# One core, a gated hybrid layer: attention heads handled in pairs, the last projection in 256-column products

## The chip, the cores and the metric

The kernel runs on one core of one Trainium2 chip. Five engines work side by side, each through its own list of instructions in order: TensorE (PE in the profile) multiplies matrices into PSUM, VectorE (DVE), ScalarE (ACT) and GpSimd (POOL) do everything elementwise, and SyncE (SP) issues the transfers. They wait for one another through semaphores. The metric is the device time of one execution in microseconds (us).

## The reference

One layer on a sequence of 256 tokens with 1024 features. Cut to what the change touches: an attention of 8 heads with 128 features each (256 keys make one block, so every query sees its own block, causally), and the last projection.

```python
h = _rmsnorm(x, norm_w) * (1 + scale) + shift
(qa, ka, va, za, qm, km, vm, zm, om, ig, fg, ga, gm) = jnp.split(h @ w_in, SPLIT_IDX, axis=-1)
...
logit_own = jnp.einsum('bhqd,bhjd->bhqj', qc, k_own) * scale + bias_own
logit_own = jnp.where(dist_own >= 0, logit_own, NEG_INF)
p = jax.nn.softmax(...)
o = jnp.einsum('bhqj,bhjd->bhqd', p_own, v_own)
...
ya = (ya * jax.nn.silu(za)) @ w_att_proj
...
y = jax.nn.sigmoid(ga) * ya + jax.nn.sigmoid(gm) * ym
return x + gate * (y @ w_out)
```

The other branch, `ym`, is a chunked linear recurrence (mLSTM) with its own projection.

## The kernel before, in words

**The stream of products.** After a first phase that normalizes x and makes the columns of q and k (line 198), everything is one loop over 100 steps, `for g in range(NG)` at line 950. Four steps make one chunk of 344 or 512 output columns; step g multiplies two of the eight blocks of 128 input features. A weight w is split into a high and a low part in the format fp32r (`split`, line 441: ACT copies `wh`, DVE subtracts `wl`), and so is the activation, and each block takes three products: high by high, high by low, low by high. In "ws" chunks (lines 1001 to 1008) the weight is the stationary operand and 256 tokens are streamed, 24 products a step. In "tok" chunks (lines 994 to 999) the activation is stationary and 512 weight columns (344 for v) are streamed, 12 products a step. At the top of step g the parts of step g+4 are made; the ring of `wh` and `wl` has five buffers each.

**The attention in between.** It is put into the stream as calls hooked to steps. `between(g, ...)` runs a call inside `split` at step g, after the copy of `wh` and ahead of the subtraction of `wl`; `at(g, ...)` runs it after that. All their TensorE work stands ahead of the step's own products. For head h, with A0 = 10:

- `att_qk` (line 599), step 10+h: q times k in plain fp32 into an `aux` tile, then DVE adds the bias `Tb` and takes the row's extreme.
- `att_exp` (line 614), step 10+h: two exponentials on ACT.
- `att_norm` (line 620), step 11+h: DVE divides by the sums.
- `att_PT` (line 626), step 13+h: three 128x128 transposes on TensorE, and ACT copies them to `PT`.
- `att_av` (line 634), two heads a call, at steps 18, 20, 21 and 22: probabilities times v in fp32; then DVE multiplies by silu(za), and ACT and POOL split the result.

`aux` has four PSUM buffers, used in turn; a taker waits until the reader of the tile four takes earlier is done. `mm`, the products' own accumulators, has two. Each fp32 product with a 128-row operand shows as two MATMUL rows in the profile.

Steps 8 to 11 belong to the last v chunk, 12 to 19 to za, 20 to 43 to qm, km and the attention's projection; steps 44 to 67 are "tok" chunks of 512 columns. Other calls that sit in the stretch: transposes of q and k (`qk_T`) at steps 10 and 12, the mLSTM's gates at steps 10 to 21, of which `gates_T` (line 584) at step 18 transposes a tile of 36 rows.

**The last projection.** Chunk 23 (counted from 0), "out" (lines 985 to 992), multiplies y by the first 512 columns of w_out, 48 products of 512 columns over four steps. The last chunk (lines 1009 to 1018) is not in that loop: it goes by pieces, 512 columns for the first 128 tokens and two of 256 for the others, 24 products each, and each piece is evacuated (`ev_out`, line 855) and written out while the next is computed.

Of the kernel before, what the change touches and what calls it, by code (L numbers as in the profile page):

```python
# [17 lines left out]
KT = 8  # L18
AH, AD = 8, 128
# [47 lines left out]
def tile_hybrid(ctx: ExitStack, tc: tile.TileContext, x, c, params2, w_row, w_va, ada_mod, ada_gate,  # L67
                w_in, w_att_proj, w_ml_proj, w_out, out):
    nc = tc.nc
# [390 lines left out]
    def between(step, fn, *a):  # L460
        hooks_between.setdefault(step, []).append((fn, a))
# [421 lines left out]
    at(10, gates_2)  # L883
    at(12, qk_T, "k", 1)
    A0 = 10
    for h in range(AH):
        between(A0 + 1 + h, att_norm, h)
        between(A0 + h, att_qk, h)
        hooks_between.setdefault(A0 + 3 + h, []).insert(0, (att_PT, (h,)))
        at(A0 + h, att_exp, h)  # L890
    for step, fn in ((12, gates_3), (14, gates_copy), (15, gates_4), (17, gates_5), (18, gates_6), (18, gates_T),
                     (19, gates_7), (21, gates_D)):
        at(step, fn)
# [4 lines left out]
                at(s + q, lambda i, *a: conv(mmt[i], *a), C[nm, hf], hf, nm, q)  # L898
                at(s + q + 1, conv_silu, hf, nm, q)
    for q in range(2):  # L900
        at(done("za", 0) + 2 + 2 * q, att_av, 2 * q)
        at(done("za", 1) + 1 + q, att_av, 4 + 2 * q)
    s = 4 * C["zm", 0]
    for half in range(2):
        at(s + 5 * half, ml_split, half)
# [44 lines left out]
    for g in range(NG):  # L950
        ci, kp = divmod(g, 4)
        ch = chunks[ci]
        if g + A < NG:
            split(g + A, hooks_between.get(g, []))
            consumed.update(li for li in cons.get(g + A, []) if li not in gate_loads)
        if kp == 0:
            if ci > 0:
                pc = chunks[ci - 1]
                if pc["name"] in EV and ci - 1 != C["za", 0]:
                    EV[pc["name"]](mmt[ci - 1], pc["half"])  # L960
                elif pc["name"] == "out":
                    for t in range(2):
                        ev_out(mmt[ci - 1][:, t], pc["half"] * 512, 512, t)
            sh = [128, 2, 512] if ch["kind"] == "tok" else [128, 4, 256]
            if ci < NCH - 1:
                mmt[ci] = ps.tile(sh, F32, name="mm", bufs=2)
                if ch["kind"] == "tok":
                    mmt[ci] = mmt[ci][:, :, 0:ch["n"]]
        for fn, a in hooks.get(g, []):
            fn(*a)  # L970
        if g == A0 + AH - 1:
            ev_za(mmt[C["za", 0]], 0)
        if g in gate_left:
            consumed.add(gate_left[g])
        pump()
        if g == NG - 8:
            load_x()
        sh_, sl_ = (hTh, hTl) if ch["stat"] is None else (T[stat[ch["stat"]][0]], T[stat[ch["stat"]][1]])
        wh, wl = whl[g]
        if ci == NCH - 1:  # L980
            continue
        for kk in range(2):
            k = 2 * kp + kk
            first, last = k == 0, k == KT - 1
            if ch["name"] == "out":

                for i in (0, 1):
                    for t in range(2):
                        a = (sh_, sl_)[i][:, k, t * 128:(t + 1) * 128]
                        for w in (wh, wl)[:2 - i]:  # L990
                            nc.tensor.matmul(mmt[ci][:, t], a, w[:, kk], start=first and i == 0 and w is wh,  # L991
                                             stop=last and i == 1)
            elif ch["kind"] == "tok":
                for t in range(2):
                    a, b = sh_[:, k, t * 128:(t + 1) * 128], sl_[:, k, t * 128:(t + 1) * 128]
                    o = mmt[ci][:, t]
                    nc.tensor.matmul(o, a, wh[:, kk], start=first, stop=False)  # L997
                    nc.tensor.matmul(o, a, wl[:, kk], start=False, stop=False)  # L998
                    nc.tensor.matmul(o, b, wh[:, kk], start=False, stop=last)  # L999
            else:  # L1000
                for i in range(4):
                    cs = slice(i * 128, (i + 1) * 128)
                    o = mmt[ci][:, i]
                    nc.tensor.matmul(o, wh[:, kk, cs], sh_[:, k], start=first and i % 2 == 0, stop=False,  # L1004
                                     skip_group_check=True)
                    nc.tensor.matmul(o, wh[:, kk, cs], sl_[:, k], start=False, stop=False, skip_group_check=True)  # L1006
                    nc.tensor.matmul(o, wl[:, kk, cs], sh_[:, k], start=False, stop=last and i % 2 == 1,  # L1007
                                     skip_group_check=True)
    ci = NCH - 1
    for t, c0, n in ((0, 0, 512), (1, 0, 256), (1, 256, 256)):  # L1010
        pt = ps.tile([128, n], F32, name="mm", bufs=2)
        for k in range(KT):
            a, b = T["yh"][:, k, t * 128:(t + 1) * 128], T["yl"][:, k, t * 128:(t + 1) * 128]
            wh, wl = (w[:, k % 2, c0:c0 + n] for w in whl[4 * ci + k // 2])
            nc.tensor.matmul(pt, a, wh, start=k == 0, stop=False)  # L1015
            nc.tensor.matmul(pt, a, wl, start=False, stop=False)  # L1016
            nc.tensor.matmul(pt, b, wh, start=False, stop=k == KT - 1)  # L1017
        ev_out(pt, 512 + c0, n, t)


# [51 lines left out]
```

## Time and profile before

| | |
|---|---|
| three timed runs | 351.73, 352.65 and 352.78 us, median 352.65 |
| the profiled execution's own time | 351.62 us |
| its span, first to last instruction | 349.8 us |
| DVE, ACT, POOL busy | 246.5, 213.4, 91.6 us |
| from HBM | 76.14 MB, 221 GB/s over the span |

All times in the profile are counted from the span's start. The timeline lists start, duration, engine, line, operation, written and read tiles, and shape; rows of the same kind that follow one another are merged with their count (x2). A matmul's end is modelled, so durations of TensorE overlap: a 256-column product is shown with 0.28 us though the next one starts 0.11 us later. What a product costs is therefore read from the distance between starts, and this "pace" is used throughout.

### The profile page before, as it was taken

The numbers are of one execution on the slowest core, as the hardware profiler recorded it, in microseconds if no ns is written. First come the engines' busy times: TensorE is split into PE (matmuls) and PEld (weight loads), VectorE is DVE, ScalarE is ACT, GpSimd is POOL, SyncE is SP. The second block draws the span as 40 slices with busy tenths as digits, with TensorE's granted clock in tenths as the row PEclk, the third lists the DMA queues.
The fourth block names the chain that finished last, engine by engine and source line by source line (L and its number), as shares of the span: only waits on it lengthen the run. The fifth ranks groups of instructions, "written<-read, shape, count | busy, mean of one in ns | idle before, by whom it ended". The sixth has DMA issues, their size and how long they took to land.

```text
span 349.8 us, 6030 instructions
## 1 busy us (share of the span) xinstructions
PE 344.9 (99%) x2360; PEld 320.0 (91%) x2360; DVE 246.5 (70%) x369; ACT 213.4 (61%) x331; POOL 91.6 (26%) x81
## 2 busy tenths in 40 slices
PE   8999999999999999999999999999999999999996
PEld 7887889999999999999998888888899999999885
DVE  6999987976994436868866693864565875479951
ACT  4868789799777867676645654446556365534410
POOL 4800003941203362455004442000011320551000
PEclk9999999999999999999999999999999999999999
DMA  8999999990661544483975737559129129291011
GB/s 301 417 415 413 416 417 420 248 356 3 227 255 62 185 176 167 145 351 123 352 250 174 308 121 249 233 192 379 31 55 379 47 89 371 84 307 54 2 60 60
DMA packets 23515, 77.77 MB, mean 222 GB/s; under 512 B 3000, under 2 KB 4928, under 8 KB 22848
## 3 DMA queue, kind: packets, MB, share of 16 engines
q1 hardware_dynamic: 23336, 76.87, 59.5%
q10 hardware_dynamic: 152, 0.53, 0.5%
q8 instruction: 18, 0.29, 0.3%
q14 instruction: 9, 0.07, 0.1%
HBM read 76.14 MB, written 1.25 MB: 221 GB/s over the span
## 4 chain that ended last, share of the span: by engine, by line
PE 98%; ACT 1%; POOL 0%; DVE 0%; issue 0%; POOLq 0%
PE mm L1007 15%; PE mm L1006 15%; PE mm L1004 15%; PE pm L198 13%; PE mm L997 8%; PE mm L998 8%; PE mm L999 8%; PE mm L991 3%; PE xps L263 1%; PE mm L1017 1%; PE mm L1015 1%; PE aux L642 1%; PE mm L1016 1%; PE aux L492 1%; PE aux L604 1%; PE aux L762 1%
## 5 line engine op out<-in xcount | busy, mean ns | idle before, releaser
L452 DVE TENSOR_TENSOR wl<-raw,wh 128x1024 fp32r<-128x1024 f32 (+1 forms) x92 | 118.2, 1296 | 64.5 <-ACT wh L448 64.5
L448 ACT CAST wh<-raw 128x1024 fp32r<-128x1024 f32 (+1 forms) x100 | 100.5, 1014 | 54.8 <-PE mm L999 25.1
L1004 PE MATMUL mm<-hTh,wh 128*128 128x256 f32 x320 | 90.0, 281 | 0.0
L1006 PE MATMUL mm<-hTl,wh 128*128 128x256 f32 x320 | 88.7, 277 | 0.0
L1007 PE MATMUL mm<-hTh,wl 128*128 128x256 f32 x320 | 88.7, 277 | 0.0
L1004 PEld LDWEIGHTS mm<-hTh,wh 128*128 128x128 f32 x320 | 60.3, 188 | 0.0
L1006 PEld LDWEIGHTS mm<-hTl,wh 128*128 128x128 f32 x320 | 60.2, 188 | 0.0
L1007 PEld LDWEIGHTS mm<-hTh,wl 128*128 128x128 f32 x320 | 60.1, 188 | 0.0
L997 PE MATMUL mm<-wh,hTh 128*128 128x512 f32 (+1 forms) x144 | 53.0, 368 | 0.0
L998 PE MATMUL mm<-wl,hTh 128*128 128x512 f32 (+1 forms) x144 | 52.6, 365 | 0.0
L999 PE MATMUL mm<-wh,hTl 128*128 128x512 f32 (+1 forms) x144 | 52.6, 365 | 0.0
L999 PEld LDWEIGHTS mm<-wh,hTl 128*128 128x128 f32 x144 | 27.0, 188 | 3.8
L997 PEld LDWEIGHTS mm<-wh,hTh 128*128 128x128 f32 x144 | 27.1, 188 | 3.6
L998 PEld LDWEIGHTS mm<-wl,hTh 128*128 128x128 f32 x144 | 27.1, 188 | 3.5
L452 POOL TENSOR_TENSOR wl<-raw,wh 128x1024 fp32r<-128x1024 f32 x8 | 19.5, 2459 | 18.4 <-ACT wh L448 12.1
L183 ACT CAST wrh<-raw 128x512 fp32r<-128x512 f32 (+1 forms) x24 | 18.2, 761 | 7.4 <-DMA raw<-in_w_row_dram 7.4
L188 DVE TENSOR_TENSOR wrl<-raw,wrh 128x512 fp32r<-128x512 f32 (+1 forms) x26 | 20.5, 811 | 1.0 <-ACT wrh L183 1.0
L198 PE MATMUL pm<-wrh,hTh 128*128 128x512 f32 x64 | 19.9, 392 | 0.0
L198 PE MATMUL pm<-wrh,hTl 128*128 128x512 f32 x64 | 19.9, 392 | 0.0
L198 PE MATMUL pm<-wrl,hTh 128*128 128x512 f32 x64 | 18.9, 394 | 0.0
L1007 PE MATMUL mm<-yah,wl 128*128 128x256 f32 x64 | 17.7, 276 | 0.0
L1004 PE MATMUL mm<-yah,wh 128*128 128x256 f32 x64 | 17.7, 276 | 0.0
(218 smaller groups left out, 644.6 us busy)
## 6 DMA issues: line engine op xcount, KB each, us to landing
raw<-in_w_in_dram SPq DMA_DIRECT2D x32, 1024.0 KB, 5.2
adat<-in_ada_mod_dram SPq DMA_DIRECT2D x16, 512.0 KB, 8.8
raw<-in_w_va_dram SPq DMA_DIRECT2D x6, 688.0 KB, 9.2
raw<-in_ada_gate_dram SPq DMA_DIRECT2D x4, 1024.0 KB, 6.2
raw<-in_w_att_proj_dram SPq DMA_DIRECT2D x4, 1024.0 KB, 5.0
raw<-in_w_ml_proj_dram SPq DMA_DIRECT2D x4, 1024.0 KB, 5.4
raw<-in_w_out_dram SPq DMA_DIRECT2D x4, 1024.0 KB, 6.3
raw<-in_w_row_dram SPq DMA_DIRECT2D x15, 256.0 KB, 8.1
```

Of the source, the lines that this page charges most:

```text
L183: copy(wsp[k][0][:, c0:c1], wrow[k][:, c0:c1])
L188: e.tensor_tensor(l[:, cs], wrow[k][:, cs], h[:, cs].bitcast(F32), op=OP.subtract)
L198: nc.tensor.matmul(pm[ch][:, t], a[:, k, t * 128:(t + 1) * 128], b[:, cs], start=k == 0 and i == 0, stop=k == KT - 1 and i == 2)
L448: nc.scalar.copy(h, w)
L452: e.tensor_tensor(l, w, h.bitcast(F32), op=OP.subtract)
L991: nc.tensor.matmul(mmt[ci][:, t], a, w[:, kk], start=first and i == 0 and w is wh, stop=last and i == 1)
L997: nc.tensor.matmul(o, a, wh[:, kk], start=first, stop=False)
L998: nc.tensor.matmul(o, a, wl[:, kk], start=False, stop=False)
L999: nc.tensor.matmul(o, b, wh[:, kk], start=False, stop=last)
L1004: nc.tensor.matmul(o, wh[:, kk, cs], sh_[:, k], start=first and i % 2 == 0, stop=False, skip_group_check=True)
L1006: nc.tensor.matmul(o, wh[:, kk, cs], sl_[:, k], start=False, stop=False, skip_group_check=True)
L1007: nc.tensor.matmul(o, wl[:, kk, cs], sh_[:, k], start=False, stop=last and i % 2 == 1, skip_group_check=True)
```

## The change

Three edits.

1. The heads go in pairs. For h = 0, 2, 4, 6 both heads' `att_qk` and `att_exp` come at step 10+h, both `att_norm` at step 11+h, both `att_PT` at step 14+h; where transposes and new q-k products share a step, the transposes come first.
2. `att_av` is called for heads 0 to 3 at step 20 and for 4 to 7 at step 22 (before: 18, 20, 21, 22).
3. In the last projection, each product of 512 streamed columns becomes two of 256, into the two halves of the same bank.

```diff
     A0 = 10
-    for h in range(AH):
-        between(A0 + 1 + h, att_norm, h)
-        between(A0 + h, att_qk, h)
-        hooks_between.setdefault(A0 + 3 + h, []).insert(0, (att_PT, (h,)))
-        at(A0 + h, att_exp, h)
+    for h in range(0, AH, 2):
+        for fn, d in ((att_PT, 4), (att_qk, 0), (att_norm, 1)):
+            for hh in (h, h + 1):
+                between(A0 + h + d, fn, hh)
+        for hh in (h, h + 1):
+            at(A0 + h, att_exp, hh)
+    for i in range(A0 + 4, A0 + AH + 4, 2):
+        hooks_between[i].sort(key=lambda f: f[0] is not att_PT)
...
     for q in range(2):
-        at(done("za", 0) + 2 + 2 * q, att_av, 2 * q)
-        at(done("za", 1) + 1 + q, att_av, 4 + 2 * q)
+        at(done("za", 1), att_av, 2 * q)
+        at(done("za", 1) + 2, att_av, 4 + 2 * q)
...
                 for i in (0, 1):
-                    for t in range(2):
+                    for t, c0 in ((0, 0), (0, 256), (1, 0), (1, 256)):
                         a = (sh_, sl_)[i][:, k, t * 128:(t + 1) * 128]
+                        cs = slice(c0, c0 + 256)
                         for w in (wh, wl)[:2 - i]:
-                            nc.tensor.matmul(mmt[ci][:, t], a, w[:, kk], start=first and i == 0 and w is wh,
-                                             stop=last and i == 1)
+                            nc.tensor.matmul(mmt[ci][:, t, cs], a, w[:, kk, cs],
+                                             start=first and i == 0 and c0 == 0 and w is wh,
+                                             stop=last and i == 1 and c0 > 0, skip_group_check=True)
...
-            wh, wl = (w[:, k % 2, c0:c0 + n] for w in whl[4 * ci + k // 2])
-            nc.tensor.matmul(pt, a, wh, start=k == 0, stop=False)
...
+            for c1 in range(0, n, 256):
+                wh, wl = (w[:, k % 2, c0 + c1:c0 + c1 + 256] for w in whl[4 * ci + k // 2])
+                o = pt[:, c1:c1 + 256]
+                nc.tensor.matmul(o, a, wh, start=k == 0 and c1 == 0, stop=False, skip_group_check=True)
...
```

On TensorE, ahead of the products of step 13, one head's transposes and one head's q-k product stood in a row (three transposes of head 0 from its probabilities `P`, then the two products of head 3):

```order
L1007 MATMUL mm_952<-hTh_70,wl_818 128x256
L629 MATMUL aux_1000<-ident_65,P_877 128x128
L630 MATMUL aux_1000<-ident_65,P_877 128x128
L631 MATMUL aux_1000<-ident_65,P_877 128x128
L604 MATMUL aux_1008<-kT_629,qT_600 128x256
L605 MATMUL aux_1008<-kT_629,qT_600 128x128
L1004 MATMUL mm_952<-hTh_70,wh_854 128x256
```

Now step 13 has none of it, and ahead of the products of step 14 stand two heads of each (0 and 1, then 4 and 5), with four `aux` tiles taken in a row:

```order
L1012 MATMUL mm_959<-hTh_70,wl_855 128x256
L629 MATMUL aux_1045<-ident_65,P_877 128x128
L630 MATMUL aux_1045<-ident_65,P_877 128x128
L631 MATMUL aux_1045<-ident_65,P_877 128x128
L629 MATMUL aux_1050<-ident_65,P_884 128x128
L630 MATMUL aux_1050<-ident_65,P_884 128x128
L631 MATMUL aux_1050<-ident_65,P_884 128x128
L604 MATMUL aux_1055<-kT_629,qT_600 128x256
L605 MATMUL aux_1055<-kT_629,qT_600 128x128
L604 MATMUL aux_1062<-kT_629,qT_600 128x256
L605 MATMUL aux_1062<-kT_629,qT_600 128x128
L1009 MATMUL mm_959<-hTh_70,wh_870 128x256
```

At step 18 TensorE had one head's transposes, the gates' two transposes of 36 rows (L587), and the first two heads of probabilities times v:

```order
L631 MATMUL aux_1245<-ident_65,P_1106 128x128
L587 MATMUL aux_1256<-ident_65,GE_1114 128x36 x2
L642 MATMUL aux_1263<-PT_873,vat_729 128x256
L644 MATMUL aux_1263<-PT_873,vat_729 128x128
L642 MATMUL aux_1263<-PT_873,vat_729 128x256
L644 MATMUL aux_1263<-PT_873,vat_729 128x128
L1004 MATMUL mm_1163<-hTh_70,wh_1044 128x256
```

Now the step's own products follow the gates' transposes directly; the products with v have gone to step 20, behind the transposes of heads 6 and 7:

```order
L631 MATMUL aux_1248<-ident_65,P_1065 128x128
L587 MATMUL aux_1256<-ident_65,GE_1112 128x36 x2
L1009 MATMUL mm_1170<-hTh_70,wh_1042 128x256
```

In the out chunk, each stationary block of y (`yh`, `yl`) was followed by 512-column products; a block of input features took these rows on TensorE:

```order
L991 MATMUL mm_3544<-wh_3402,yh_3406 128x512
L991 MATMUL mm_3544<-wl_3403,yh_3406 128x512
L991 MATMUL mm_3544<-wh_3402,yh_3406 128x512
L991 MATMUL mm_3544<-wl_3403,yh_3406 128x512
L991 MATMUL mm_3544<-wh_3402,yl_3407 128x512 x2
```

Now it takes twice as many of half the width, the same stationary block loaded for each:

```order
L995 MATMUL mm_3544<-wh_3402,yh_3406 128x256
L995 MATMUL mm_3544<-wl_3403,yh_3406 128x256
L995 MATMUL mm_3544<-wh_3402,yh_3406 128x256
L995 MATMUL mm_3544<-wl_3403,yh_3406 128x256
...
L995 MATMUL mm_3544<-wh_3402,yl_3407 128x256 x4
```

More of the change, by code (lines that the diff above doesn't have):

```diff
@@ L1013, in tile_hybrid @@
             a, b = T["yh"][:, k, t * 128:(t + 1) * 128], T["yl"][:, k, t * 128:(t + 1) * 128]
-            wh, wl = (w[:, k % 2, c0:c0 + n] for w in whl[4 * ci + k // 2])
-            nc.tensor.matmul(pt, a, wh, start=k == 0, stop=False)
-            nc.tensor.matmul(pt, a, wl, start=False, stop=False)
-            nc.tensor.matmul(pt, b, wh, start=False, stop=k == KT - 1)
+            for c1 in range(0, n, 256):
+                wh, wl = (w[:, k % 2, c0 + c1:c0 + c1 + 256] for w in whl[4 * ci + k // 2])
+                o = pt[:, c1:c1 + 256]
+                nc.tensor.matmul(o, a, wh, start=k == 0 and c1 == 0, stop=False, skip_group_check=True)
+                nc.tensor.matmul(o, a, wl, start=False, stop=False, skip_group_check=True)
+                nc.tensor.matmul(o, b, wh, start=False, stop=k == KT - 1 and c1 + 256 == n, skip_group_check=True)
         ev_out(pt, 512 + c0, n, t)
```

## The prediction

> **What bounds the kernel now.** I read the page first, then TensorE's waits, then the timeline of TensorE row by row.
>
> ```profile
> span 349.8 us, 6030 instructions
> PE 344.9 (99%) x2360; PEld 320.0 (91%) x2360; DVE 246.5 (70%) x369; ACT 213.4 (61%) x331; POOL 91.6 (26%) x81
> PEclk9999999999999999999999999999999999999999
> PE 98%; ACT 1%; POOL 0%; DVE 0%; issue 0%; POOLq 0%
> PE warm L227 <- POOL ident masks.py:199: 1.4, 1, 1.4
> PE xps L263 <- ACT diag L246: 0.2, 1, 0.2
> ```
>
> The first four rows are the page's: TensorE is busy for 99% of the span, at 90% or more of its clock in every slice, and it holds 98% of the chain that ended last. The last two are the whole answer on TensorE's waits: 1.6 us, both in the first microseconds. So no attention call and no weight split is waited for longer than the view can show; the time is the sum of the distances between TensorE's starts. A change pays only if it shortens those, or costs if it makes TensorE wait. Busy time says nothing here, since modelled ends overlap; I use starts.
>
> **The last projection.** The rows are starts from the timeline, and groups with their counts.
>
> ```profile
> 324.12 0.39 PE L991 MATMUL mm<-wh,yh 128*128 128x512 f32 x1
> 340.88 0.28 PE L1015 MATMUL mm<-wh,yh 128*128 128x256 f32 x1
> 346.21 0.28 PE L1017 MATMUL mm<-wh,yl 128*128 128x256 f32 x1
> L991 PE MATMUL mm<-wh,yh 128*128 128x512 f32 x16 | 6.3, 394 | 0.0
> L1015 PE MATMUL mm<-wh,yh 128*128 128x512 f32 x8 | 3.1, 393 | 0.0
> L1015 PE MATMUL mm<-wh,yh 128*128 128x256 f32 x16 | 4.4, 276 | 0.0
> 211.34 0.40 PE L997 MATMUL mm<-wh,hTh 128*128 128x512 f32 x1
> 244.00 0.28 PE L779 MATMUL aux<-vaug,SD 128*128 128x258 f32 x1
> L997 PE MATMUL mm<-wh,hTh 128*128 128x512 f32 x48 | 18.7, 389 | 0.0
> ```
>
> Each group row is one of three alike (high by high, low, high), so between 324.12 and 340.88 lie 3 x 16 + 3 x 8 = 72 products of 512 columns: 16.76 / 72 = 0.2328 us each. From 340.88 to 346.21 the last two pieces start 3 x 16 = 48 products of 256 columns, 47 distances: 5.33 / 47 = 0.1134 us each. These take the same `wh`, `wl`, `yh` and `yl` tiles as the piece before, so the nearest row for the new form is in this very stage: two halves at 0.2268 against 0.2328. The last three rows say that 512 columns need not be slower: in the longest uninterrupted run of them, 3 x 48 = 144 products take 32.66 us, 0.2268 each, exactly two halves. The out stage is off that pace by 0.006, for a reason that the trace doesn't name. **Saving: 72 x 0.006 = 0.43 us**, all of it on the path, since nothing but TensorE holds the end there. Between ends: halves also run at a worse pace, 0.118 (shown below), which would give 0.236 a pair and 72 x 0.0032 = 0.23 us lost. I take the tail's row, the nearest.
>
> The Trainium skill, "TensorE: Matmul & The Clock Gate", Back-to-back issue gap, speaks against this edit: alone, a warm matmul's gap is N / 2.4 ns and about 2.5 ns more, whatever the width; so 72 more products would cost 72 x 2.5 ns = 0.18 us by it, an estimate. The rows above do not agree: 0.1134 is more than its 0.109, and twice it is no more than a whole. That rule's result is a rival below, priced from rows.
>
> **The attention's groups.** Thirteen steps, 10 to 22, have fp32 work ahead of their products; afterwards seven have (10, 12, 14, 16, 18, 20, 22). The number of products and transposes is the same, so only what each change of kind costs can go. Step 19 shows it alone, three transposes and 24 products:
>
> ```profile
> 109.36 0.27 PE L629 MATMUL aux<-ident,P 128*128 128x128 f32 x1
> 109.47 0.27 PE L630 MATMUL aux<-ident,P 128*128 128x128 f32 x1
> 109.58 0.27 PE L631 MATMUL aux<-ident,P 128*128 128x128 f32 x1
> 109.61 0.37 PE L1004 MATMUL mm<-hTh,wh 128*128 128x256 f32 x1
> 109.81 0.28 PE L1006 MATMUL mm<-hTl,wh 128*128 128x256 f32 x1
> 112.43 0.27 PE L629 MATMUL aux<-ident,P 128*128 128x128 f32 x1
> ```
>
> Transposes stand 0.11 apart. The last is followed after only 0.03, and the first product takes 0.20 in place of 0.1134: 0.08 early, 0.09 late. Read singly the 0.20 looks like a stop of 0.09 at each return to the stream, thirteen times; taken together it is mostly a matter of where the start is stamped. The whole step takes 112.43 - 109.36 = 3.07 us against 3 x 0.11 + 24 x 0.1134 = 3.05. **One group costs 0.02 us, six fewer save 0.12.** The ends: nothing, if the 0.02 is rounding, and 6 x 0.09 = 0.54, if the 0.20 is a stop after all.
>
> Step 18 is the one group with more:
>
> ```profile
> 104.76 0.27 PE L631 MATMUL aux<-ident,P 128*128 128x128 f32 x1
> 104.96 0.31 PE L587 MATMUL aux<-ident,GE 36*128 36x36 f32 x2
> 105.20 0.70 PE L642 MATMUL aux<-PT,vat 128*128 128x256 f32 x2
> 105.74 0.38 PE L644 MATMUL aux<-PT,vat 128*128 128x128 f32 x2
> 104.39 0.42 ACT L565 ACTIVATE GE<-G 4x256 f32<-4x256 f32 x1 [0.88 <-DVE st L622]
> 116.89 0.59 PE L642 MATMUL aux<-PT,vat 128*128 128x256 f32 x2
> 117.33 0.39 PE L644 MATMUL aux<-PT,vat 128*128 128x128 f32 x2
> ```
>
> The gates' transposes start 0.20 after L631 rather than 0.11, right after ACT ended L565 at 104.81: a wait of 0.09. They then hold 0.24, and the first pair of L642 takes 0.54, where in step 21 (116.89 to 117.33) it takes 0.44. The products with v leave this place, the gates' transposes stay. L565 hangs on DVE work of step 17, which now has no q-k product to wait for, but two heads to normalize; it comes as late relative to TensorE, I judge. So 0.09 of wait stays, and the 0.10 behind goes or moves to the step's own products. I count 0, with the ends 0.19 gained and 0.1 lost (the wait twice as long).
>
> On this the Trainium skill, "TensorEngine Tiling (Array Packing)", Key Properties, says that a change of tiling mode drains TensorE. Only L587 has 36 rows; by that rule the entry and the exit are paid before and after alike, which is the 0 that I count.
>
> **What the moves could make late.** No moved call issues a DMA. POOL gets the gates' copy and masks ahead of the first `yal`, which the projection at step 36 needs. What TensorE needs of the moved calls comes earlier: transposes of a pair follow its products by four steps, where each head had three.
>
> ```profile
> 84.93 0.28 DVE L624 TENSOR_SCALAR P<-P,st 128x128 f32<-128x128 f32 x1
> 89.62 0.27 PE L629 MATMUL aux<-ident,P 128*128 128x128 f32 x1
> 75.50:125.00 49.50, 49.50 (x397) 48.46 (x396) 33.95 (x80) 39.75 (x79) 14.69 (x14) 1.00 0.45 161
> ```
>
> Head 1 was normalized at 85.2 and transposed at 89.62, 4.4 us later, with three steps between; with four it has a step (2.8 us) more, less the other head's 0.8 on DVE and 0.9 on ACT. The four `aux` tiles of step 14 were last read two steps before. The last row (length; busy us of PE, its weight loads, DVE, ACT, POOL) has DVE busy for 34 and ACT for 40 of 49.5 us, so two heads at a time fit. **Cost: 0.** If that cover were gone, each microsecond of a late tile would stop all that is queued behind on TensorE, one for one.
>
> **The sum.** -0.43 - 0.12 = -0.55 us: 351.62 becomes 351.07 for the profiled execution (span 349.8 to about 349.25, with the same 1.82 around it). That execution is 1.03 below the median of the three runs; against 352.65 the forecast is **352.1 us**.
>
> **A term that can't be summed: the pace after a group.**
>
> ```profile
> 268.61 0.28 PE L1006 MATMUL mm<-hTl,wh 128*128 128x256 f32 x1
> 276.97 0.60 PE L816 MATMUL aux<-ident,omt 128*128 128x128 f32 x4
> 122.37 0.28 PE L1006 MATMUL mm<-hTl,wh 128*128 128x256 f32 x1
> 182.11 0.40 PE L997 MATMUL mm<-wh,hTh 128*128 128x512 f32 x1
> 86.91 0.28 PE L1006 MATMUL mm<-hTl,wh 128*128 128x256 f32 x1
> ```
>
> After the group that ends at 268.41, 71 products take 8.36 us, 0.1177 each, until the next group; after the one of step 22, 527 take 59.74, 0.1134. Same form, nothing waited for: the stream falls into one of two paces when it is re-entered, a close one and a wide one, and keeps it. Step 13 (86.91 to 89.62, 23 products) has the wide pace too, at 0.1178. Of the eleven 256-column steps 12 to 22, I read three as wide throughout (12, 13, 20). A wide step costs 24 x 0.0043 = 0.10 us. With new groups the draw is new: all three going close would gain 0.3 (and up to 0.1 more in the v chunk), three more wide steps lose as much. I count 0.
>
> **The rivals.**
> - *The wide pace catches the long run.* After step 22 there is no other group until step 47 and the width stays the same through 22 steps. If this entry falls on the wide side and stays there, 22 x 0.10 = 2.2 us are lost: 354.3. For it: about one entry in four is wide, and 72 products in a row never healed. Against it: this very entry was close, as were most with products with v before it. It decides from six wide steps (0.55 / 0.10), and ends clearly slower from sixteen. Chance 0.10.
> - *The halves run at the wide pace*: +0.23 for -0.43, so 352.65 + 0.23 - 0.12 = 352.8. For it: the 512-column products of this stage are off pace now. Against it: the tail's 47 distances, on the same tiles. 0.12.
> - *Each product has a price of its own*, the rule above. Rows bound it: a half at 0.1134 and a whole at 0.2268 leave 0.0001 at most, 72 x 0.0001 = 0.01 us; if the out stage's 0.006 is owed to something else and stays, the sum is +0.01 - 0.12: 352.5. 0.08.
> - *The groups cost nothing*, and pairing does not do what fewer groups suggest: only -0.43, 352.2. 0.15.
> - *The gain is larger*: a stop of 0.09 at each return (-0.54 in place of -0.12) or the wide steps gone (-0.4): 351.65. 0.13.
> - The forecast itself, 352.1: 0.42.
>
> **How the numbers follow.** A measurement of this kernel tells about 0.3%, 1.06 us, from no change. The forecast is half of that. The four executions shown, all of one kernel, lie in two pairs one microsecond apart (351.62 and 351.73, 352.65 and 352.78), so a median can fall on either, and that alone carries part of the forecast's chance to "faster": 0.12 of its 0.42 and the near rivals, and 0.08 of the larger gain, 0.20. Slower is the long run's 0.10 and 0.01 of the rest. The range goes from the larger gain on the lower of the pairs, 351.0, to the halves' rival on a high one, 353.2; the long run at the wide pace (0.10) and the far low end stay outside.
>
> **What would show each step.** In the new profile the first L995 to the last piece's first product should span 16.3 us, not 16.76, with pairs 0.227 apart; at 0.236 the second rival holds. From the first product of step 10's group to the end of step 22, 0.1 to 0.2 us should go, with steps 11, 13, 15, 17, 19 and 21 free of any 0.20. TensorE's waits should still list the first two rows alone; a third one, on ACT or DVE between 75 and 125 us, proves the cover wrong. And the distance from step 22's first product to the first 512-column product should be 59.9 us; 62 is the wide pace. The prediction is wrong if the time leaves the range, and wrong in its reasons if the out stage does not shorten.

## The result and the profile after

The changed kernel takes **355.09 us** (median of 22 runs, 352.77 to 358.0), the kernel before 351.88 beside it (22 runs, 351.3 to 353.14): ratio 1.0076, 95% interval 1.006 to 1.0092. It is slower by 0.8%, where 352.1 was forecast. The profiled execution took 355.62 us, 4.0 more than that of before.

These rows answer to the first ones shown of before: two of the page, then all that the view of TensorE's waits holds (microseconds in total, times, longest).

```profile
span 353.8 us, 6176 instructions
PE 347.2 (98%) x2432; PEld 325.2 (92%) x2432; DVE 246.5 (70%) x369; ACT 212.8 (60%) x331; POOL 90.0 (25%) x81
```

```profile
PE aux L587 <- ACT GE L565: 1.7, 1, 1.7
PE warm L227 <- POOL ident masks.py:199: 1.4, 1, 1.4
PE xps L263 <- ACT diag L246: 0.3, 1, 0.3
```

A third wait has come: TensorE stops for 1.7 us ahead of the gates' transposes of step 18. That is less than half of 4.0, so I cut the span at starts. First the row of before that the prediction did not show, then the timeline of TensorE after, with the start and the modelled length in front.

```profile
75.50 0.38 PE L604 MATMUL aux<-kT,qT 128*128 128x256 f32 x1
```

```profile
75.88 0.38 PE L604 MATMUL aux<-kT,qT 128*128 128x256 f32 x1
104.88 0.27 PE L631 MATMUL aux<-ident,P 128*128 128x128 f32 x1
106.83 0.31 PE L587 MATMUL aux<-ident,GE 36*128 36x36 f32 x2 [1.68 <-ACT GE L565]
107.07 0.39 PE L1009 MATMUL mm<-hTh,wh 128*128 128x256 f32 x1
124.32 0.36 PE L1009 MATMUL mm<-hTh,wh 128*128 128x256 f32 x1
186.59 0.39 PE L1002 MATMUL mm<-wh,hTh 128*128 128x512 f32 x1
328.60 0.28 PE L995 MATMUL mm<-wh,yh 128*128 128x256 f32 x1
350.25 0.28 PE L1024 MATMUL mm<-wh,yl 128*128 128x256 f32 x1
```

| stretch | before | after | difference |
|---|---|---|---|
| start to step 10's group | 75.50 | 75.88 | +0.38 |
| from there to the first product after step 22's group | 46.67 | 48.44 | +1.77 |
| the 528 products of steps 22 to 43 (the long run) | 59.94 | 62.27 | +2.33 |
| step 44 to the out stage | 142.01 | 142.01 | 0 |
| out stage, first to last product | 22.09 | 21.65 | -0.44 |
| behind the last product | 3.59 | 3.58 | -0.01 |

The first row is start-up, which lies between 75.40 and 76.19 us in the eighteen profiles, all of programs that are alike there. Two things cost: a stop, and a wider pace (62.27 / 528 = 0.118 us per product in place of 0.1135). The halves gained what was forecast.

**Why the stop.** L587 transposes `GE`, which ACT writes at L565. These are ACT's rows around it, then DVE's.

```profile
101.48 0.51 ACT L616 ACTIVATE P<-P,st 128x256 f32<-128x256 f32 x1 [1.80 <-DVE st L608]
102.87 0.39 ACT L617 ACTIVATE P<-P,st 128x128 f32<-128x128 f32 x1
103.26 1.03 ACT L448 CAST wh<-raw 128x1024 fp32r<-128x1024 f32 x1
106.36 0.41 ACT L565 ACTIVATE GE<-G 4x256 f32<-4x256 f32 x1 [2.07 <-DVE G L564]
```

```profile
100.39 0.68 DVE L559 TENSOR_TENSOR_SCAN G<-GE 4x256 f32<-4x256 f32 x1
100.99 0.39 DVE L608 CUSTOM_DVE_ANT_0 P<-aux,Tb 128x256 f32<-128x256 f32 x1
104.33 0.28 DVE L624 TENSOR_SCALAR P<-P,st 128x128 f32<-128x128 f32 x1
104.53 1.22 DVE L452 TENSOR_TENSOR wl<-raw,wh 128x1024 fp32r<-128x1024 f32 x1
105.66 0.27 DVE L563 TENSOR_SCALAR G<-G 4x256 f32<-4x256 f32 x1
105.86 0.41 DVE L564 TENSOR_TENSOR G<-G 4x256 f32<-4x256 f32 x1
```

Followed backwards: L565 waits 2.07 us for DVE's L564. That stands in DVE's order behind a weight split (L452, 1.22 us) and the norms of two heads (the last at 104.33). The split needs the cast that ACT starts at 103.26, behind the exponentials of two heads (from 101.48), and these need DVE's L608, issued behind a scan of the gates. The view by windows has the length, then busy time and count of PE, its weight loads, DVE, ACT and POOL, then the granted clock (and the DMA's share and rate):

```profile
95.30:105.90 10.60, 9.85 (x84) 9.51 (x82) 10.04 (x29) 7.15 (x20) 0.00 (x0) 1.00 0.78 296
```

DVE is busy for 10.04 of these 10.60 us, so what stands in front of L564 delays it in full, and two heads' work stands where one head's stood. L565 starts 1.97 us later than before (104.39), while TensorE comes only 0.12 later (104.88 against 104.76), after a start-up that was 0.38 later.

**Why the times spread.** Before spans 1.8 us, the changed kernel 5.2. Each execution comes with its mean granted clock, and times and clocks together make four groups:

| long run | mean clock 0.998 to 1.0 | mean clock 0.993 to 0.995 |
|---|---|---|
| close pace | 7 runs, 352.77 to 353.79 | 3 runs, 353.92 to 354.12 |
| wide pace | 8 runs, 355.04 to 356.19 | 4 runs, 356.87 to 358.0 |

Close and wide are told by time here; the two executions of this program with a profile (355.62 above, and 352.77 in an experiment below) bear it out. So 12 of 22 went at the wide pace, and 7 of 22 had a clock that was reduced for a while; the median is a wide run.

### The profile page after: what moved, and what is told of

Its sections match the earlier page's. It is cut to its first block, busy times and chain, and to the rows that moved or that the text cites. A ratio compares the mean times of both kernels' runs of the same rounds, so it can differ in the third digit from the quotient of the medians.

```text
span 353.8 us, 6176 instructions
## 1 busy us (share of the span) xinstructions
PE 347.2 (98%) x2432; PEld 325.2 (92%) x2432; DVE 246.5 (70%) x369; ACT 212.8 (60%) x331; POOL 90.0 (25%) x81
## 4 chain that ended last, share of the span: by engine, by line
PE 95%; DVE 2%; ACT 1%; issue 0%; POOL 0%; POOLq 0%; DVEq 0%; ACTq 0%
PE mm L1009 14%; PE mm L1011 14%; PE mm L1012 14%; PE pm L198 13%; PE mm L1002 8%; PE mm L1003 8%; PE mm L1004 8%; PE mm L995 3%; PE xps L263 1%; PE mm L1024 1%; PE mm L1023 1%; PE mm L1022 1%; DVE wl L452 1%; PE aux L492 1%; PE aux L642 1%; PE aux L762 1%
## 5 line engine op out<-in xcount | busy, mean ns | idle before, releaser
L452 DVE TENSOR_TENSOR wl<-raw,wh 128x1024 fp32r<-128x1024 f32 (+1 forms) x92 | 117.6, 1290 | 66.4 <-ACT wh L448 66.3
L452 POOL TENSOR_TENSOR wl<-raw,wh 128x1024 fp32r<-128x1024 f32 x8 | 19.5, 2457 | 19.0 <-ACT wh L448 19.0
```

The lines of the kernel that those rows point to most:

```text
L452: e.tensor_tensor(l, w, h.bitcast(F32), op=OP.subtract)
```

## The experiments

Steps are counted as in the prediction. All ratios are to the kernel before, run on the same chip beside it. "Close" and "wide" say how the long run was in the profile.

| kernel | median (range; runs) | ratio, interval | steps 10-22 | long run | out stage |
|---|---|---|---|---|---|
| halves alone (e1) | 351.88 (351.28-352.74; 11) | 0.9995, 0.9984-1.0007 | 46.68 | 59.95 | 21.65 |
| attention alone (e2) | 354.93 (353.99-357.3; 6) | 1.0092, 1.0066-1.0118 | 48.24 | 62.27 | 22.09 |
| gates' transposes at 20 (e3) | 354.46 (353.12-356.22; 6) | 1.008, 1.0056-1.0103 | 46.66 | 59.94 | 21.72 |
| pairs, v as before (e4) | 353.63 (352.57-355.16; 10) | 1.0037, 1.0014-1.0061 | 48.06 | 59.95 | 21.65 |
| the changed kernel again (g1) | 352.77 (1) | | 48.24 | 59.94 | 21.65 |
| before, gates at 17 (g2) | 356.3 (356.07-357.51; 4) | 1.0129, 1.0103-1.0154 | 52.52 | 59.94 | 22.09 |
| a group at step 24 (g3) | 353.45 (352.85-356.2; 10) | 1.0065, 1.004-1.009 | 48.22 | 60.28 | 21.65 |
| e4 with gates at 20 (g4) | 352.52 (352.38-352.75; 10) | 1.0016, 1.0007-1.0026 | 46.31 | 59.95 | 21.72 |
| gates_5 at 16 (h1) | 353.72 (353.4-354.58; 6) | 1.0051, 1.0033-1.0068 | 46.69 | 62.27 | 21.65 |
| e4 with gates_5 at 16 (h2) | 351.26 (350.67-352.54; 12) | 0.9989, 0.9975-1.0003 | 46.31 | 59.95 | 21.65 |
| e1 with gates at 20 (h3) | 350.99 (350.86-351.32; 10) | 0.9975, 0.9965-0.9984 | 46.68 | 59.95 | 21.65 |
| g4 with a group at 78 (h4) | 352.78 (352.61-353.73; 10) | 1.0029, 1.0017-1.0041 | 46.31 | 59.95 | 21.72 |
| single heads, v as changed (k1) | 353.86 (353.58-353.9; 5) | 1.0042, 1.0023-1.0062 | 46.96 | 62.27 | 21.65 |
| h1, last v call alone (k2) | 351.2 (351.06-352.14; 10) | 0.9979, 0.9969-0.999 | 46.60 | 59.95 | 21.65 |
| h1 again (k3) | 353.89 (1) | | 46.69 | 62.27 | 21.65 |
| e3 again (k4) | 355.75 (1) | | 46.85 | 62.27 | 21.72 |

### The halves alone (e1)

The attention lines are those of before; the last projection is the changed one.

```diff
-    for h in range(0, AH, 2):
...
+    for h in range(AH):
+        between(A0 + 1 + h, att_norm, h)
+        between(A0 + h, att_qk, h)
+        hooks_between.setdefault(A0 + 3 + h, []).insert(0, (att_PT, (h,)))
+        at(A0 + h, att_exp, h)
...
-        at(done("za", 1), att_av, 2 * q)
-        at(done("za", 1) + 2, att_av, 4 + 2 * q)
+        at(done("za", 0) + 2 + 2 * q, att_av, 2 * q)
+        at(done("za", 1) + 1 + q, att_av, 4 + 2 * q)
```

> The attention of before, only the last projection in halves. Theory A (the loss sits in the attention's stretch alone; the halves run at the close pace): the out stage spans 16.3 us instead of 16.76, TensorE's waits list the first two rows alone, the time is 0.44 us below before, 351.4. Rival B (more, smaller products cost time somewhere, for instance by the pace they are left in): same as before or up to 0.2 us more.

The timeline of TensorE has the first and the last product of the out stage:

```profile
324.83 0.28 PE L992 MATMUL mm<-wh,yh 128*128 128x256 f32 x1
346.48 0.28 PE L1021 MATMUL mm<-wh,yl 128*128 128x256 f32 x1
```

The stage takes 21.65 against 22.09: -0.44, shown on the path. The median moved by 0.24 us, which is no measured difference: the interval includes 1, and the runs spread over 1.46 us. No wait at L587, long run close.

### The attention alone (e2)

The loops of the last projection are those of before, in whole 512-column products.

```diff
-                    for t, c0 in ((0, 0), (0, 256), (1, 0), (1, 256)):
+                    for t in range(2):
...
-            for c1 in range(0, n, 256):
```

> Only the attention edits, the last projection as before. Theory A: the loss of the whole change and the 0.44 us of the halves on top: a wait of 1.7 to 1.9 us at the gates' transposes (L587) of step 18, and in some executions a long run of 62.3 us in place of 59.9, so 353.2 where the long run is close and 355.5 where it is wide. Rival B: if the halves were part of the loss, this is nearer to before than the changed kernel is.

The stop (1.7 us) and the wide long run are both there: the whole loss belongs to the attention's edits.

### The gates' transposes two steps later (e3), and again (k4)

```diff
-    for step, fn in ((12, gates_3), (14, gates_copy), (15, gates_4), (17, gates_5), (18, gates_6), (18, gates_T),
+    for step, fn in ((12, gates_3), (14, gates_copy), (15, gates_4), (17, gates_5), (18, gates_6), (20, gates_T),
```

> The changed kernel, with the gates' transposes called at step 20 instead of 18, between the transposes of heads 6 and 7 and the products with v. Theory A (TensorE stops because its list holds, at step 18, an instruction whose input the late ACT and DVE finish 1.9 us after it): the wait vanishes, steps 10 to 22 are about 1.8 us shorter, and the time is 351.0 where the long run is close, 353.3 where it is wide. Rival C (ACT and DVE are late as a whole, so that another instruction is waited for instead): a new row of 1 us or more in TensorE's waits, and the time stays within 0.5 us of the changed kernel.

> The changed kernel with the gates' transposes at step 20, once more for a second profile; its six times lay from 353.12 to 356.22. Theory N: both long runs as in the first profile (59.9 us, and 143.5 us from step 44 to the out stage), 353.1 to 354. Rival O: the first run at 62.3 us, 355 to 356.5.

The stop is gone in both: steps 10 to 22 take 46.66 and 46.85. The time did not follow, for two reasons. The 384 products ahead of the out stage turned wide (step 44 to the out stage 143.49 in place of 142.01), and the long run differs between two executions of one program. Its first and last starts, in the first profile and in the second:

```profile
122.58 0.37 PE L1009 MATMUL mm<-hTh,wh 128*128 128x256 f32 x1
182.51 0.40 PE L1002 MATMUL mm<-wh,hTh 128*128 128x512 f32 x1
```

```profile
122.90 0.36 PE L1009 MATMUL mm<-hTh,wh 128*128 128x256 f32 x1
185.17 0.39 PE L1002 MATMUL mm<-wh,hTh 128*128 128x512 f32 x1
```

59.93 and 62.27 us. So the pace can differ between two executions of one program, and it needs no stop to be wide.

### Pairs, with the products with v where they were (e4)

```diff
-        at(done("za", 1), att_av, 2 * q)
-        at(done("za", 1) + 2, att_av, 4 + 2 * q)
+        at(done("za", 0) + 2 + 2 * q, att_av, 2 * q)
+        at(done("za", 1) + 1 + q, att_av, 4 + 2 * q)
```

> The changed kernel with the products with v at their old steps (18, 20, 21, 22; two heads at a time), the pairs of heads kept. Theory A: the wait at L587 stays, 1.7 to 1.9 us, so 352.8 at the least. For the pace of the long run: if the form of the last group ahead of it decides (one call of two heads as before, 8 MATMUL rows, instead of 16), the long run is 59.9 us in all executions and the times lie together at 352.8; if it is drawn by the moment at which TensorE comes out of its wait, it is wide in about half of them and the times spread up to 355.3.

The stop stays (1.7 us, `L631` to `L587` 1.954), the long run is close. So the stop belongs to the pairs and not to the products with v. The times still spread over 2.6 us; the four highest, 354.11 to 355.16, are those with a mean clock of 0.995, the other six have 1.0.

### The changed kernel again (g1)

> The changed kernel once more, for a second profile. Theory D (the pace of the long run of 528 products after step 22 is drawn anew in each execution, and the two clusters of its times, near 352.9 and near 355.3, are the two draws): either the long run is 59.9 us and the execution's time 352.8 to 354, or 62.3 us and 355 to 356.5; the wait at L587 is 1.7 us both times. Rival E (the program fixes the pace; the clusters come from elsewhere, the start for instance): 62.3 us again whatever the time is.

Step 10's group and the long run, from its timeline of TensorE:

```profile
75.54 0.38 PE L604 MATMUL aux<-kT,qT 128*128 128x256 f32 x1
123.78 0.37 PE L1009 MATMUL mm<-hTh,wh 128*128 128x256 f32 x1
183.71 0.40 PE L1002 MATMUL mm<-wh,hTh 128*128 128x512 f32 x1
```

The long run takes 59.93 here and took 62.27 in the first profile: same program, same stop (1.7), other pace. 355.62 - 352.77 = 2.85 us between the two is 2.34 of pace, 0.34 of start-up and 0.2 in steps 10 to 22.

That 0.2 tells where the two part. These are the first product behind step 20's group and the first row of step 22's group, in the first profile and in g1; 48 products lie between.

```profile
116.04 0.37 PE L1009 MATMUL mm<-hTh,wh 128*128 128x256 f32 x1
121.78 0.60 PE L642 MATMUL aux<-PT,vat 128*128 128x256 f32 x2
```

```profile
115.70 0.37 PE L1009 MATMUL mm<-hTh,wh 128*128 128x256 f32 x1
121.24 0.59 PE L642 MATMUL aux<-PT,vat 128*128 128x256 f32 x2
```

5.74 against 5.54 us: steps 20 and 21 are already wide in the one and close in the other, and up to step 19 the paces are alike. So the pace of the long run is settled at step 20, two steps before the long run starts. The two profiles of e3's program part at the same place (5.54 us in e3, 5.74 in k4).

### Before, with the gates' transposes too early (g2)

A stop of known size, made in the kernel before, with one att_av call ahead of the long run.

```diff
-    for step, fn in ((12, gates_3), (14, gates_copy), (15, gates_4), (17, gates_5), (18, gates_6), (18, gates_T),
+    for step, fn in ((12, gates_3), (14, gates_copy), (15, gates_4), (17, gates_5), (17, gates_T), (18, gates_6),
```

> The kernel before, heads one at a time and products of 512 as they were, with the gates' transposes called at step 17, right behind the work they need, so that TensorE has to wait there as in the changed kernel. Theory F (what costs is an early place for L587, not the pairs; and a true wait draws the pace anew): a wait of about 3 us, 3 us over before at the least, and times that spread over more than 2 us. Rival G (the wait alone costs its own length, the pace belongs to the pairs): 3 us over before, the times within 1.5 us of one another, the long run 59.9 us.

The long run stayed close (59.94), so a stop doesn't make it wide. But steps 10 to 22 took 5.85 us more, for a distance that grew by 3.180 - 0.203 = 2.98. The timeline of TensorE, then the list of cores:

```profile
101.64 0.38 PE L605 MATMUL aux<-kT,qT 128*128 128x128 f32 x2
104.93 0.42 PE L587 MATMUL aux<-ident,GE 36*128 36x36 f32 x2 [2.91 <-ACT GE L565]
105.66 0.41 PE L1006 MATMUL mm<-hTl,wh 128*128 128x256 f32 x1
105.88 0.42 PE L1007 MATMUL mm<-hTh,wl 128*128 128x256 f32 x1
```

```profile
core 0: 355.7 us, clock 0.990
```

Products behind the stop stand 0.21 apart, not 0.113, and the mean clock is 0.990. The next rows are windows again; the granted clock is the figure behind POOL's.

```profile
102.00:104.00 2.00, 0.03 (x1) 0.00 (x0) 1.94 (x7) 1.37 (x6) 0.00 (x0) 1.00 0.06 25
104.40:111.20 6.80, 6.27 (x29) 6.20 (x30) 0.85 (x4) 3.33 (x4) 0.00 (x0) 0.50 0.28 80
```

2.4 us after the last product ended, with TensorE still stopped, the clock fell to 0.50 and stayed there for 6.8 us: **a stop of 2.9 us was paid twice**, 2.98 for itself and 2.87 for the work behind it at half speed. The other three runs have a mean clock of 0.995: 0.005 x 354 us / 0.5 = 3.5 us at half, half as long, and they are 1.1 to 1.4 us faster. All four had it, so the cost was 4.5 us (356.3 against 351.83) where both theories said 3 or more.

### A group of fp32 work inside the long run (g3)

Three transposes of the identity, read by nobody, are added at step 24.

```diff
+    def extra_group():
+        pa = aux([128, 384])
+        for q in range(3):
+            nc.tensor.transpose(pa[:, q * 128:(q + 1) * 128], ident, ident)
+
+    at(24, extra_group)
```

> The changed kernel with three more transposes (of the identity, read by nobody) ahead of step 24, 48 products into the long run. They cost 0.35 us themselves. Theory H (the pace is set when the stream is re-entered, so a further entry draws again, and one behind transposes alone was close in step 19 of before): the rest of the long run is at 0.1134, also where the part before it is at 0.118, and the times lie together near 353.2 to 354. Rival I (the wide pace comes from what ACT and DVE do meanwhile): no change of pace at step 24, and the times spread as in the changed kernel, 0.35 us higher.

Inconclusive: in this profile the long run was close before the group already (60.28, with 0.35 for the group). Of the ten runs, the four from 354.75 up have a mean clock of 0.994 to 0.995. The six at full clock all lie from 352.85 to 353.52, where 8 of 15 such runs of the changed kernel are wide; with the same odds that would happen once in a hundred times ((7/15) to the sixth). It leans towards theory H here, but no profile shows a wide run that turns close.

### Pairs, v as before, and the gates at step 20 (g4); a group at step 78 (h4)

g4 joins the edits of e3 and e4. h4 adds to it the group of three transposes, read by nobody:

```diff
+    at(78, extra_group)
```

> The changed kernel's pairs and halves, the products with v at their old steps, the gates' transposes at step 20 behind heads 6 and 7. Theory A: no wait at L587, steps 10 to 22 take 46.3 us (46.67 before), the out stage is 0.44 us shorter, so 351.0 if both long runs of 256-column products (22 steps after step 22, 16 steps ahead of the out stage) fall on the close pace; 353.3 or 352.7 where the first or the second does not. Rival C (lateness is only handed on): a new wait of 1 us or more.

> The kernel with pairs, old places of the products with v and the gates' transposes at step 20, whose second long run was wide (143.5 us from step 44 to the out stage) with times within 0.4 us; here with three more transposes of the identity ahead of step 78, two steps into that run. Theory H (the pace is set at each entry, and can be set anew by one more): the run after step 78 at 0.1134, 142.5 us for the stretch, times together near 351.6. Rival: it stays at 0.118, and the time is 0.35 us above that kernel, 352.9.

Without stop and with a close long run the times of g4 lie within 0.37 us. It is still no faster than before, since the 384 products ahead of the out stage are wide:

```profile
280.02 0.36 PE L1009 MATMUL mm<-hTh,wh 128*128 128x256 f32 x1
325.33 0.28 PE L995 MATMUL mm<-wh,yh 128*128 128x256 f32 x1
```

45.31 us, 0.118 each. In h4 the stretch from step 44 to the out stage stayed wide through the added entry (143.82 with the group; g4 143.49). So in this second run another group does not bring the close pace back; there theory H fell.

### gates_5 one step earlier (h1), and again (k3); with v as before (h2)

```diff
-    for step, fn in ((12, gates_3), (14, gates_copy), (15, gates_4), (17, gates_5), (18, gates_6), (18, gates_T),
+    for step, fn in ((12, gates_3), (14, gates_copy), (15, gates_4), (16, gates_5), (18, gates_6), (18, gates_T),
```

> The changed kernel with the gates' fifth part (two DVE operations and the exponential L565) called at step 16 instead of 17; the gates' transposes stay at step 18. Theory A (L565 is late because on DVE its input stands behind the two normalizations and a weight's low part of step 17, which themselves wait for ACT): the wait at L587 vanishes, steps 10 to 22 take 46.5 to 46.7 us, the time is 350.9 to 351.2 where both long runs are close, up to 2.3 or 1.5 more where one is wide. Rival C (everything on ACT and DVE is late): the wait shrinks by less than half, or comes back at another row.

> As the kernel before it in this list, and the products with v at their old steps. Theory A: steps 10 to 22 take 46.3 us, 350.9 where both long runs are close. It is the version that could beat both kernels. Rival: a wide pace in one of the runs, fixed by the program as in the kernel with the gates' transposes at step 20, which gives 352.4 to 353.2 with little spread.

> The changed kernel with the fifth part at step 16, once more for a second profile. Theory N (without a wait the program fixes the pace): the long run is 62.3 us again, 353.4 to 354.6. Rival O (it is drawn by the start of the execution): 59.9 us is possible, then 351.1 to 352.2.

DVE, ACT and TensorE in h1:

```profile
103.29 0.41 DVE L564 TENSOR_TENSOR G<-G 4x256 f32<-4x256 f32 x1
103.79 0.42 ACT L565 ACTIVATE GE<-G 4x256 f32<-4x256 f32 x1 [0.57 <-DVE st L622]
104.75 0.27 PE L631 MATMUL aux<-ident,P 128*128 128x128 f32 x1
104.95 0.31 PE L587 MATMUL aux<-ident,GE 36*128 36x36 f32 x2
```

L564 now stands ahead of the two heads' norms and the weight split, `GE` is ready at 104.21, and the stop is gone, though DVE has the same work to do: the stop was a matter of DVE's order. All six runs of h1, and k3, still lie at 353.4 or above, and both profiles have the wide long run (62.27). h2, with v as before, has neither fault: 0.9989 (0.9975 to 1.0003), not told from before (in the profile its start-up was 0.58 us later than that of before).

### Single heads, with the gates at step 20 (h3)

e1 with `(20, gates_T)`, to see whether that edit alone turns the products ahead of the out stage wide, as it did in e3, k4, g4 and h4.

> Heads one at a time as before, halves in the last projection, and the gates' transposes at step 20. Theory J (where TensorE never truly waits, its own list fixes the pace of the runs that follow, and it is the moved transposes that put the second long run, 16 steps ahead of the out stage, on the wide pace): that run at 0.118 again, the stretch from step 44 to the out stage 143.5 us, times together near 352.8. Rival K (the pairs do it): 142.0 us, 351.4.

It does not: step 44 to the out stage takes 141.71. Of the kernels with the gates at step 20, only those with pairs have a wide second run. This is the fastest of all (0.9975, 0.9965 to 0.9984), and its gain is 0.30 there and 0.44 in the out stage. The 0.30 are the 72 products that the prediction showed at 0.1177, which take 8.27 us here and 8.57 before; they are close in k1 too, so it needs no gates at step 20.

### The products with v alone (k1), and the last call alone (k2)

k1 is e1 with the changed places of v: two att_av calls at step 20, two at step 22. k2 is h1 with

```diff
-        at(done("za", 1) + 2, att_av, 4 + 2 * q)
+        at(done("za", 1) + 1 + q, att_av, 4 + 2 * q)
```

so that step 21 and step 22 have one call each.

> Heads one at a time as before, halves in the last projection, and the new places of the products with v: two calls at step 20, two at step 22. Theory L (the two calls in the last group put the long run of 528 products at risk): the run takes 62.3 us in the profile or in part of the executions, with times up to 353.6, although nothing waits at L587. Rival M (pairs of heads or the wait do it): 59.9 us, the times within 1.5 us of one another near 351.2.

> Pairs, halves and the gates' fifth part at step 16; the products with v of heads 0 to 3 at step 20, those of 4 and 5 at step 21, those of 6 and 7 alone at step 22. Theory L: the long run is close, 59.9 us, no wait at L587, steps 10 to 22 in 46.3 to 46.6 us, 350.9 to 351.9. Rival M: 62.3 us as in the kernel with both calls at step 22, 353.4 and more.

First and last start of the long run in k1, then in k2:

```profile
122.87 0.36 PE L1006 MATMUL mm<-hTh,wh 128*128 128x256 f32 x1
185.14 0.39 PE L999 MATMUL mm<-wh,hTh 128*128 128x512 f32 x1
```

```profile
122.28 0.36 PE L1009 MATMUL mm<-hTh,wh 128*128 128x256 f32 x1
182.22 0.40 PE L1002 MATMUL mm<-wh,hTh 128*128 128x512 f32 x1
```

62.27 and 59.94. The long run can be wide without any pair or stop when two calls stand ahead of it. Over all profiles: one call, close in 9 of 9; two calls, wide in 6 of 9. Steps 20 and 21 tell which: behind two calls the long run had the pace of these two steps in 9 of 9, wide or close. Behind one call it was close whatever had come before; in k2 step 20 is wide, and the single call of step 21 ends it:

```profile
114.08 0.37 PE L1009 MATMUL mm<-hTh,wh 128*128 128x256 f32 x1
117.00 0.60 PE L642 MATMUL aux<-PT,vat 128*128 128x256 f32 x2
118.23 0.37 PE L1009 MATMUL mm<-hTh,wh 128*128 128x256 f32 x1
121.05 0.59 PE L642 MATMUL aux<-PT,vat 128*128 128x256 f32 x2
```

24 products take 2.92 us in step 20 and 2.82 in step 21. So the changed kernel's two calls at step 22 do not make the long run wide; they keep what step 20 had. k2 is the changed kernel with its two faults taken away, and it beats before (0.9979, 0.9969 to 0.999).

**The clock and the stop.** The kernels with the stop at L587 (the changed kernel with g1, e2, e4, g3 and g2) have mean clocks of 0.990 to 0.995 in 21 of their 53 runs. The eleven experiments without it have none below 0.998 in 82 runs, and the kernel before has two among 83. In the changed kernel that costs 1.2 us (354.04 against 352.86, medians of the close groups) to 2.0 (357.29 against 355.34, the wide ones). Where the clock falls within the work is seen in g2's profile alone; of the others no profile caught such an execution, so that it falls behind the stop of 1.7 us is inferred from these counts. Two more profiles show how long a stop it takes: in e2 and g4 the clock fell 2.0 and 2.2 us after TensorE's last product had ended. That is at the end of the program, where it costs nothing, and it is why their mean clocks are 0.998.

## Why the prediction was wrong, step by step

- **What bounds the kernel**: right. Starts of TensorE account for the whole difference, and no busy share shows it.
- **The last projection**, -0.43: right, -0.44 in all kernels with halves but four (21.65); in those, with pairs and the gates at step 20, it is -0.37 (21.72). The rivals on a wide pace for the halves and on a price per product fell.
- **Step 18**: the first of two steps that failed. "It comes as late relative to TensorE, I judge" was counted 0 with ends of 0.19 gained and 0.1 lost; it cost 1.75 us (1.95 less the 0.20 that the distance always was). I had looked at DVE's and ACT's sums over 49.5 us ("two heads at a time fit"). They hide that DVE is busy for 95% of the 10.6 us that end with L564, and say nothing of who stands ahead of L564 in DVE's order. h1 shows that the order was the cause.
- **"A wait of 0.09"** at L587 was no wait. The distance is 0.203 or 0.204 in e3, g4, h2 and h3 as well; in h1 `GE` was ready 0.74 us ahead, and it is 0.20. It is what going into the 36-row form takes here. The Trainium skill, "TensorEngine Tiling (Array Packing)", Key Properties, says that a change of tiling mode drains TensorE; no run here shows whether 36 rows are such a change.
- **Cost: 0** for what the moves make late: its own test, a third row of waits between 75 and 125 us, came. The price one for one was right for the stop itself; a reduced clock, which no rival held, adds 1.2 to 2.0 us in 7 of 22 runs.
- **The pace after a group**: the second step that failed, and in the profiled execution the larger. It was counted 0, with the rival that the wide pace catches the long run at 0.10. That rival came in 12 of 22 runs, and its 2.2 us measured 2.33. "This very entry was close" was no argument, since the change puts two att_av calls where one was. And the rival had the place wrong: not the entry at step 22 decides but the one at step 20, and two calls keep what one call would have ended (k2). Its time, 354.3, lies 1.0 below the median of the wide runs at full clock (355.34): it lacks the stop's 1.75, and it starts from a median of three runs, 352.65, that is 0.77 above the 351.88 that before took in 22.
- **The groups**, -0.12: mis-sized and mixed with pace. Where there is no stop, pairs with v as before give 46.31 in steps 10 to 22 (h2, g4): -0.36. Four heads of v at a time give back 0.38 with pairs (h1 46.69) and cost 0.28 with single heads (k1 46.96 against e1 46.68). Most of this is pace. Before has three wide steps in this stretch (12, 13 and 20), h2 and g4 none, h1 four (18 to 21), and k1 six (12, 13 and 18 to 21) where e1 has three. At 0.10 a step that is 0.3 of the -0.36, 0.4 for h1 and 0.3 for k1, so some 0.06 is left for the groups themselves.

**The sum** by what was measured, from the profile before to the one after: start-up 0.38, the stop 1.75, the rest of steps 10 to 22 0.02, the long run 2.33, the halves -0.44, the tail -0.01: +4.0.

**What stays open.** What in TensorE sets the pace is not settled. Shown is no more than this: entries have two outcomes, the one at step 20 can differ between two executions of one program, and of the two forms of group at step 22 one keeps the pace and the other ends with the close one. Nor is it known why the gates at step 20 turn the second run wide with pairs and not with single heads.

## What to carry to other kernels

Before moving work in a kernel whose bound engine never waits, follow each late operand back through the order of the engines that make it, row by row, and in the microseconds ahead of it: a free share of 30% on DVE over the span did not prevent a stop of 1.7 us, since just there DVE was 95% busy, and moving one small call a step earlier removed it. Weigh a stop of some microseconds on TensorE at more than its length, since the clock may fall (here in all four runs with a stop of 2.9 us, and in 17 of 49 with one of 1.7). Time such a kernel over many runs and sort them by time and mean clock: of the two profiles of the changed kernel one took 352.8 us and the other 355.6.

## What the hardware showed that was not expected

- One program runs 528 products of 256 columns in 59.94 or in 62.27 us, at full clock, with no wait shown, and keeps its pace through the whole run. The pace also passes through a last group that has 16 rows with v and nothing else (9 of 9 profiles), while behind such a group of 8 it was close (9 of 9).
- The clock fell to 0.50 after 2.4 us of a stop and stayed there for 6.8 us in one profile; behind the last product it fell after 2.0 us in another (e2). The Trainium skill, "TensorE: Matmul & The Clock Gate", What's actually happening, has these two states and a free-running window of about 3.4 us; by that figure, an estimate, 6.8 us are two windows, and the 3.5 us behind a mean of 0.995 are one. By that section an idle window of about 3.4 us comes first; here 2.0 us was enough, and kernels with stops of 1.7 us had a reduced mean clock in part of their runs. Whether the phase of the window decides in which runs, no run shows.
- Entering the 36-row transposes takes 0.20 us even with everything ready, and the first of the products with v behind them 0.54 in place of 0.44.
